# A short-convolution layer: a pinned start with adaLN in pairs of tiles, another plan of passes, sums seeded in PSUM, 1024-wide evictions

## The chip, the cores and the metric

The kernel runs on one core of a Trainium2 chip. The metric is the time of one execution in microseconds on the device. The core has TensorE (PE, with its weight loads shown apart as PEld), VectorE (DVE), ScalarE (ACT), GpSimd (POOL) and SyncE (SP, whose queue issues nearly all loads). The engines run their own instruction streams in order and wait for each other by semaphores.

## What is computed

One layer with depth 1, so only the short gated convolution is used. D is 2048 features, E 4096 channels, 256 tokens, all in float32.

```python
h = rmsnorm(x, norm_g[0])
mod = silu(c) @ ada_w[0] + ada_b[0]              # 2048 x 6144
shift, scale, gate = split(mod, 3)
h = h * (1 + scale) + shift
b_gate, c_gate, v, g = split(h @ sc_w_in[0], 4)  # 2048 x 16384
u = causal_depthwise_conv(c_gate * v, sc_conv_w[0])   # width 3
y = b_gate * u * silu(g)
out = rmsnorm(x + gate * (y @ sc_w_out[0]), final_g)  # 4096 x 2048
```

## The kernel before, in words

**Products.** PE multiplies in a form that takes numbers of reduced width in one pass (`fp32r`). To keep the exactness of float32, each operand is split into two parts that sum to it: `split` makes `hi` on ACT (a cast) and `lo = raw - hi` on DVE for every piece of weights, and the tokens lie in `hT` as a high half `hh_` and a low half `hl_`. A product of a 128 x 128 block of weights and 256 tokens is then three matmuls: `hi` with `hh`, `hi` with `hl`, `lo` with `hh`. They are called products here.

**The start.** x is loaded by token tiles, normalised, and turned by PE (`tp_x`) so that its features lie on partitions, in `xs`. adaLN's shift and scale are a product of a single vector with a 2048 x 4096 matrix. It is done on DVE: a piece of `ada_w` (`at`) is multiplied by `silu_c`, one number per partition, and added to `gv` (L236, L238); then PE turns `gv` (`tp_g`, L247), ACT sums along the rows (L249), and DVE makes `scale` and `shift` (L251 to L253). Features come in 16 tiles of 128. `ADA` lists how many tiles' columns come together. When a group's scale and shift are known, `xs` is modulated (L258) and split into `hT` (L261, L262).

**First stage.** So that PE has work while adaLN's matrix streams in, the first 16 channel tiles are cut along the contraction: 4 chunks of 4 channel tiles, each with its four quarters of `w_in` (the order is `QUARTERS`). A call of `part` is one pass: it takes, for one chunk and quarter, the products of feature tiles `k0` to `k1`, collected in two banks `mm_s`, and copies the sum to `acc` (ACT, L298) or adds it there (DVE, L300). `plan()` writes down the order of passes and of adaLN's pieces before anything runs, from a count of loads and products. Before the change it gives 56 passes, 16 of them first ones and 40 that add.

**Second stage.** The other 16 channel tiles go two at a time over all features: `mm_b`, where one matmul takes `hi` with both halves of a feature tile's tokens (512 wide, L382) and a second `lo` with `hh` (L385). Gate columns of `ada_w` (`at_g`) are summed meanwhile. **Third stage.** The product with `w_out` (`mm_o`, L426 to L428), four chunks of 512 columns, each for two token tiles, then the gated residual (`gated`) and the last norm (`finish`). In the last chunk three pieces' products of the second token tile are put off (`late`), so that the first tile's residual and norm run beside them.

**What sets the order.** Python's order gives priorities; a scheduler with a model of the engines' times then sets each engine's order and the semaphores. Tiles come from pools with a fixed number of buffers (`raw` 3, `hi` and `lo` 3 each, `at` 4, PSUM `mm` 6 banks and `sm` 2), and a load waits on SP's queue until its buffer is free; what stands behind it on the queue waits too.

Of the kernel before, what the change touches and what calls it, by code (L numbers as in the profile page):

```python
# [13 lines left out]
P = 128  # L14
# [8 lines left out]
# Channel tiles whose products are cut along the contraction, while the adaLN vectors stream in: NCH chunks of  # L23
# CT tiles, each chunk in its four quarters of w_in; the feature tiles that adaLN's vectors come in.
# [7 lines left out]
BEHIND = 20  # L32
DELAY = 80
PRODUCTS = 1.7
# Numbers per partition of a piece of w_in or w_out and of a piece of ada_w; slots of CT * T numbers.
# [4 lines left out]

def plan():
    """The order of the start: ("ada", k0, nk, i) loads the i-th piece of the columns of adaLN's feature tiles k0 to
    k0 + nk, ("mm", chunk, quarter, k0, k1) takes the products of feature tiles k0 to k1 for a part of the channels.
    A unit is the load of one 128 x 128 block."""
    steps, ready = [], []
    parts = [(ch, q) for ch in range(NCH) for q in QUARTERS]
    done = {p: 0 for p in parts}
    pieces = [(sum(ADA[:g]), nk, i) for g, nk in enumerate(ADA) for i in range(4 * nk)]
    load, pe = 32.0, 0.0

    def ada():
        nonlocal load
        k0, nk, i = pieces.pop(0)
        steps.append(("ada", k0, nk, i))
        load += 8
        if i == 4 * nk - 1:
            ready.extend([load + DELAY] * nk)

    def take(p, hi):
        nonlocal load, pe  # L60
        n = (hi - done[p]) * CT
        steps.append(("mm", *p, done[p], hi))
        load += n
        pe = max(pe, ready[hi - 1], load + 16 - n) + n * PRODUCTS
        done[p] = hi

    for _ in range(4 * ADA[0]):
        ada()
    while any(done[p] < KT for p in parts):
        while pieces and load + 8 < pe - BEHIND:  # L70
            ada()
        new = [p for p in parts if done[p] == 0]
        hi = sum(r <= max(pe, ready[0]) for r in ready)
        if new:
            take(new[0], hi)
            continue
        old = [p for p in parts if done[p] < KT]
        p = old[0] if hi == KT else min(old, key=lambda p: done[p])
        if hi == done[p]:
            while len(ready) == hi:  # L80
                ada()
            pe = ready[hi]
            hi = sum(r <= pe for r in ready)
        take(p, hi)
    return steps
# [3 lines left out]
def short_conv_layer(ctx: ExitStack, tc: tile.TileContext, x, c, norm_g, ada_w, ada_b, w_in, conv_w, w_out, final_g, out):  # L89
# [6 lines left out]
    psum = ctx.enter_context(tc.tile_pool(name="psum", bufs=6, space=PSUM))  # L96
# [12 lines left out]
    rows1 = const.tile([80, P], F32, tag="rows1", name="rows1")  # L109
    rows2 = const.tile([96, P], F32, tag="rows2", name="rows2")  # L110
    nc.sync.dma_start(rows1[0:16, :], c.rearrange("o (k p) -> (o k) p", p=P))
    xt = [raw_tile(f"x{t}") for t in range(TT)]
    for t in range(TT):
        for dh in range(2):
            dd = slice(dh * (D // 2), (dh + 1) * (D // 2))
            nc.sync.dma_start(xt[t][:, dd], x[t * P : (t + 1) * P, dd])
    nc.sync.dma_start(rows1[16:32, :], norm_g.rearrange("o (k p) -> (o k) p", p=P))
    nc.sync.dma_start(rows1[32:80, :], ada_b.rearrange("o (k p) -> (o k) p", p=P))
# [8 lines left out]
    vec = const.tile([P, 80], F32, tag="vec", name="vec")  # L127
# [3 lines left out]
    def turn(rows, n, lo, dst):  # L131
        tp = psum.tile([P, 512], F32, tag="sm", name="tp_v", bufs=2)
        nc.tensor.transpose(tp[:, : n - lo], rows[lo:n, :], ident[lo:n, lo:n])
        nc.vector.tensor_copy(dst, tp[:, : n - lo])

    turn(rows1, 16, 0, vec[:, 0:16])
    silu = nc.scalar.activation(silu_c, vec[:, 0:16], AF.Silu)

    # The square root's table is fetched before the squares' sum asks for it.
    warm = const.tile([P, 1], F32, tag="warm", name="warm")  # L140
    root = nc.scalar.activation(warm, eps_t, AF.Sqrt)
    tc.add_manual_dep(root.ins, silu.ins.name, after, reason="one change of table")

# [1 line left out]
    ssq = const.tile([P, 2, TT], F32, tag="ssq", name="ssq")  # L145
    rstd = const.tile([P, TT], F32, tag="rstd", name="rstd")
    junk = hpool.tile([P, SLOT], F32, tag="big", name="junk")
    for t in range(TT):
        for dh in range(2):
            dd = slice(dh * (D // 2), (dh + 1) * (D // 2))  # L150
            sq = nc.scalar.activation(junk[:, dd], xt[t][:, dd], AF.Square, accum_out=ssq[:, dh, t : t + 1])
            tc.add_manual_dep(sq.ins, root.ins.name, after, reason="one change of table")
# [3 lines left out]
    for dh in range(2):  # L156
        dd = slice(dh * (D // 2), (dh + 1) * (D // 2))
        for t in range(TT):
            if t == 0:
                nc.scalar.activation(xt[t][:, dd], xt[t][:, dd], AF.Copy, scale=rstd[:, t : t + 1])  # L160
            else:
                nc.vector.tensor_scalar_mul(xt[t][:, dd], xt[t][:, dd], rstd[:, t : t + 1])
# [8 lines left out]
    for k in range(0, KT, 2):  # L171
        tp = psum.tile([P, 2, T], F32, tag="sm", name="tp_x", bufs=2)
        for i in range(2):
            for t in range(TT):
                nc.tensor.transpose(tp[:, i, t * P : (t + 1) * P], xt[t][:, (k + i) * P : (k + i + 1) * P], ident)
        nc.scalar.copy(xs[k // CT][:, k % CT : k % CT + 2, :], tp)
    turn(rows1, 80, 0, vec)
    gT = vec[:, 16:32]
    b_shift = vec[:, 32:48]
    b_scale = vec[:, 48:64]  # L180
    nc.sync.dma_start(rows2[:, :], conv_w.rearrange("w (k p) -> (w k) p", p=P))
    turn(rows2, 96, 0, cw)
# [3 lines left out]

    def split(raw, n):
        """raw = hi + lo, exactly, each of them a number that one pass carries."""
# [5 lines left out]

    def conv(ct, u, cv):
        """u = causal convolution of cv over time, one channel per partition."""
# [11 lines left out]

# [1 line left out]
    acc = {}  # L210
    gjunk = const.tile([P, P], F32, tag="gjunk", name="gjunk")
    adas = ada_w[0].rearrange("(k p) (s f) -> p k s f", p=P, s=3)

    sums = {}
# [298 lines left out]
```

## Time and profile before

| what | value |
|---|---|
| time, median of 3 runs | 952.5 us (952.2 to 952.86) |
| profiled execution, span from first to last instruction | 951.9 us (no other time of it is given) |
| TensorE clock granted, mean over the span | 0.989 |
| read from HBM | 224.49 MB, 238 GB/s over the span |
| PE's last product of the third stage | starts at 942.7 us |

The page gives busy times per engine and the costliest groups of instructions; a table of stretches gives, for each stretch of time, the busy time and the number of instructions of each engine, the clock that TensorE was granted (1.00 is full) and the load rate. The time between the starts of two instructions of a kind, and not their busy time, says how fast PE goes, since its matmuls overlap.

### The profile page before, as it was taken

The numbers are of one execution on the slowest core, as the hardware profiler recorded it, in microseconds if no ns is written. First come the engines' busy times: TensorE is split into PE (matmuls) and PEld (weight loads), VectorE is DVE, ScalarE is ACT, GpSimd is POOL, SyncE is SP. The second block draws the span as 40 slices with busy tenths as digits, with TensorE's granted clock in tenths as the row PEclk, the third lists the DMA queues.
The fourth block names the chain that finished last, engine by engine and source line by source line (L and its number), as shares of the span: only waits on it lengthen the run. The fifth ranks groups of instructions, "written<-read, shape, count | busy, mean of one in ns | idle before, by whom it ended". The sixth has DMA issues, their size and how long they took to land.

```text
span 951.9 us, 14329 instructions
## 1 busy us (share of the span) xinstructions
PE 917.5 (96%) x5963; PEld 834.8 (88%) x5963; DVE 667.7 (70%) x785; ACT 418.2 (44%) x468; POOL 0.7 (0%) x6
## 2 busy tenths in 40 slices
PE   3699999999999999999999999999999999999996
PEld 2699999999999999988888888888888878888884
DVE  4798998899899998997565556556555654454533
ACT  6575342443435444444443544444444433433332
POOL 0000000000000000000000000000000000000000
PEclk9799999999999999999999999999999999999998
DMA  9999997999988887886655665565556585665532
GB/s 271 298 360 368 283 337 251 326 329 321 366 296 290 256 261 237 281 298 200 198 195 178 193 203 179 185 199 190 177 184 201 191 309 180 198 198 177 180 130 88
DMA packets 172048, 227.51 MB, mean 239 GB/s; under 512 B 5792, under 2 KB 112464, under 8 KB 171600
## 3 DMA queue, kind: packets, MB, share of 16 engines
q1 hardware_dynamic: 171984, 226.61, 73.0%
q8 instruction: 46, 0.75, 0.3%
q14 instruction: 18, 0.15, 0.0%
HBM read 224.49 MB, written 2.10 MB: 238 GB/s over the span
## 4 chain that ended last, share of the span: by engine, by line
PE 90%; DMA 4%; DVE 3%; issue 1%; ACT 1%; SPq 1%; ACTq 0%; DVEq 0%
PE mm_b L382 25%; PE mm_b L385 13%; PE mm_s L292 11%; PE mm_s L286 11%; PE mm_s L291 11%; PE mm_o L427 6%; PE mm_o L426 6%; PE mm_o L428 6%; DMA raw_s<-in_sc_w_in_dram 2%; DMA at<-in_ada_w_dram 2%; DVE lo L192 1%; DMA x<-in_x_dram 1%; DVE gv L238 1%; ACT hi L191 0%; SPq L231 0%
## 5 line engine op out<-in xcount | busy, mean ns | idle before, releaser
L382 PE MATMUL mm_b<-hT,hi 128*128 128x512 f32 x1024 | 355.2, 392 | 0.0
L286 PE MATMUL mm_s<-hT,hi 128*128 128x256 f32 x1024 | 286.9, 284 | 9.2 <-ACT hT L261 4.9
L291 PE MATMUL mm_s<-hT,hi 128*128 128x256 f32 x1024 | 287.2, 283 | 0.0
L385 PE MATMUL mm_b<-hT,lo 128*128 128x256 f32 x1024 | 285.4, 280 | 0.0
L292 PE MATMUL mm_s<-hT,lo 128*128 128x256 f32 x1024 | 282.9, 283 | 1.4 <-DVE lo L192 1.3
L192 DVE TENSOR_TENSOR lo<-raw,hi 128x2048 fp32r<-128x2048 f32 x64 | 146.6, 2291 | 128.4 <-ACT hi L191 128.3
L382 PEld LDWEIGHTS mm_b<-hT,hi 128*128 128x128 f32 x1024 | 192.1, 188 | 42.3 <-issue 0.2
L191 ACT CAST hi<-raw_s 128x2048 fp32r<-128x2048 f32 (+3 forms) x85 | 126.5, 1489 | 177.5 <-PE mm_s L291 120.7
L286 PEld LDWEIGHTS mm_s<-hT,hi 128*128 128x128 f32 x1024 | 194.3, 191 | 10.2 <-ACT hT L261 5.1
L291 PEld LDWEIGHTS mm_s<-hT,hi 128*128 128x128 f32 x1024 | 195.1, 191 | 0.2 <-issue 0.2
L292 PEld LDWEIGHTS mm_s<-hT,lo 128*128 128x128 f32 x1024 | 191.9, 190 | 2.3 <-DVE lo L192 2.1
L385 PEld LDWEIGHTS mm_b<-hT,lo 128*128 128x128 f32 x1024 | 192.3, 188 | 0.5 <-issue 0.2
L191 ACT CAST hi<-raw 128x2048 fp32r<-128x2048 f32 x64 | 122.4, 1912 | 158.0 <-PE mm_b L382 103.1
L192 DVE TENSOR_TENSOR lo<-raw_s,hi 128x2048 fp32r<-128x2048 f32 (+3 forms) x85 | 149.5, 1759 | 19.7 <-ACT hi L191 19.2
L192 DVE TENSOR_TENSOR lo<-raw_o,hi 128x2048 fp32r<-128x2048 f32 x32 | 73.4, 2292 | 85.4 <-ACT hi L191 85.4
L191 ACT CAST hi<-raw_o 128x2048 fp32r<-128x2048 f32 x32 | 61.2, 1913 | 105.1 <-PE mm_o L428 92.3
L427 PE MATMUL mm_o<-lo,y 128*128 128x512 f32 x256 | 101.8, 399 | 0.0
L426 PE MATMUL mm_o<-hi,y 128*128 128x512 f32 x256 | 101.0, 396 | 0.0
L428 PE MATMUL mm_o<-hi,y 128*128 128x512 f32 x256 | 100.1, 392 | 0.0
L238 DVE SCALAR_TENSOR_TENSOR gv<-at,silu_c,gv 128x512 f32<-128x512 f32 (+1 forms) x149 | 92.2, 639 | 2.6 <-DMA at<-in_ada_w_dram 1.9
L426 PEld LDWEIGHTS mm_o<-hi,y 128*128 128x128 f32 x256 | 48.1, 188 | 12.6 <-issue 0.2
L428 PEld LDWEIGHTS mm_o<-hi,y 128*128 128x128 f32 x256 | 48.1, 188 | 11.5
(80 smaller groups left out, 441.8 us busy)
## 6 DMA issues: line engine op xcount, KB each, us to landing
raw<-in_sc_w_in_dram SPq DMA_DIRECT2D x64, 1024.0 KB, 5.6
raw_s<-in_sc_w_in_dram SPq DMA_DIRECT2D x46, 1024.0 KB, 7.5
at<-in_ada_w_dram SPq DMA_DIRECT2D x128, 256.0 KB, 6.6
raw_o<-in_sc_w_out_dram SPq DMA_DIRECT2D x32, 1024.0 KB, 5.1
at_g<-in_ada_w_dram SPq DMA_DIRECT2D x32, 512.0 KB, 6.8
raw_s<-in_sc_w_in_dram SPq DMA_DIRECT2D x19, 512.0 KB, 5.8
raw_s<-in_sc_w_in_dram SPq DMA_DIRECT2D x7, 768.0 KB, 7.6
raw_s<-in_sc_w_in_dram SPq DMA_DIRECT2D x13, 256.0 KB, 4.5
```

The costliest lines, as they stand in the source:

```text
L191: nc.scalar.copy(hi[:, :n], raw[:, :n])
L192: nc.vector.tensor_tensor(out=lo[:, :n], in0=raw[:, :n], in1=hi[:, :n].bitcast(F32), op=ALU.subtract)
L238: nc.vector.scalar_tensor_tensor(out=g2, in0=at4[:, i], scalar=c_k, in1=g2, op0=ALU.mult, op1=ALU.add)
L286: first = nc.tensor.matmul(dst, hi[:, o], hh, start=opens, stop=False, skip_group_check=True)
L291: nc.tensor.matmul(dst, hi[:, o], hl, start=False, stop=False, skip_group_check=True)
L292: nc.tensor.matmul(dst, lo[:, o], hh, start=False, stop=k == k1 - 1, skip_group_check=True)
L382: nc.tensor.matmul(banks[m].rearrange("p a t -> p (a t)"), hi[:, o], hT[:, k, :], start=k == 0, stop=False, skip_group_check=True)
L385: nc.tensor.matmul(banks[m][:, 0, :], lo[:, o], hh_[:, k], start=False, stop=k == KT - 1, skip_group_check=True)
L426: nc.tensor.matmul(po, yh, hi[:, o], start=ct == 0, stop=False)
L427: nc.tensor.matmul(po, yh, lo[:, o], start=False, stop=False)
L428: nc.tensor.matmul(po, yl, hi[:, o], start=False, stop=ct == NCT - 1)
```

## The change

- **Start.** All instructions of the start are pinned in the order in which they are written (`in_order`), and what comes behind may be tied to their ends (`behind`). The small loads of vectors go to ACT's queue. x comes first on SP, then adaLN's columns of the first two feature tiles in pieces of 4, 4, 4, 2, 1 and 1 row blocks, with the first weights ahead of the last piece. x lies in four slots of its own. Half of the squares are done on DVE. Only the first four feature tiles of x are scaled and turned in the start; the others follow behind the passes number 4, 7 and 10 (`turn_x`). `idle(n)` has PE turn `ident` n times without use between the loads' landings, 104 times in all.
- **adaLN.** Eight groups of two tiles. The sum over partitions is a matmul with a column of ones, and its result is read from PSUM; three of the first group's 16 row blocks are taken by PE instead of DVE (`ON_PE`). `hT`'s high half is made by ACT straight from `xs` with scale and bias; DVE modulates `xs` beside it for the low half.
- **Plan.** `plan()` counts in microseconds for loads, PE, DVE and ACT, and gives 51 passes: 16 first ones (12 with two feature tiles, then four with four) and 35 that add. Each says whether it is seeded; all 35 are.
- **Seeds.** A seeded pass first has ACT copy `acc` into the pass's PSUM tile, PE adds to it, and ACT copies the sum back. No DVE addition is left.
- **1024-wide tiles in PSUM.** `mm` has three tiles of two banks each, evicted by one instruction. In the third stage the two token tiles share one such tile (`both`).
- adaLN's sums and the gate's sums get a later priority (`later`).

```diff
-ADA = [1, 1, 1, 1, 2, 2, 2, 2, 2, 2]
+ADA = [2] * 8
...
+    steps, ready = [], [0.0] * ADA[0]
...
+        products((hi - done[p]) * CT, ready[hi - 1])
+        seed = done[p] > 0 and act < dve
...
-    psum = ctx.enter_context(tc.tile_pool(name="psum", bufs=6, space=PSUM))
+    psum = ctx.enter_context(tc.tile_pool(name="psum", bufs=3, space=PSUM))
...
+    @contextmanager
+    def in_order():
+        traced = nc.cur_bb.bb.instructions
+        n = len(traced)
+        yield
+        last = {}
+        for ins in list(traced[n:]):
+            if ins.engine in last:
+                tc.add_manual_dep(ins, last[ins.engine], after, reason="in order")
+            last[ins.engine] = ins.name
+        ended.update(last)
...
+    GIVE = 300
+    IDLE = (16, 30, 24, 14, 14, 6)
+    xt = [[slot([P, HX], f"x{t}{dh}") for dh in range(2)] for t in range(TT)]
...
+    nc.scalar.dma_start(rows0[:, :], c.rearrange("o (k p) -> (o k) p", p=P))
...
+    for n, (j, kk) in enumerate(((0, 4), (4, 4), (8, 4), (12, 2), (14, 1), (15, 1))):
...
+        if j == KT - 1:
+            raw0 = raw_tile("raw0")
+            first_load(raw0, 0)
+        for s in range(2):
+            nc.sync.dma_start(at[:, :, s, :], adas[:, j : j + kk, s, 0 : NK0 * P])
...
+    def idle(n):
+        for _ in range(n):
+            nc.tensor.transpose(tp_idle[:, 0, 0:P], ident, ident)
...
+    def turn_x(k0, k1, vector=False):
+        c0, n = k0 % 8 * P, (k1 - k0) * P
+        x0, x1 = (xt[t][k0 // 8][:, c0 : c0 + n] for t in range(TT))
+        nc.scalar.activation(x0, x0, AF.Copy, scale=rstd[:, 0:1])
...
+    def modulate(k0, nk, sums):
...
+            nc.vector.tensor_tensor(out=scale[:, ks], in0=sums[1], in1=b_scale1[:, ks], op=ALU.add)
+            nc.vector.tensor_tensor(out=scale[:, ks], in0=scale[:, ks], in1=gT[:, ks], op=ALU.mult)
+            nc.vector.tensor_tensor(out=shift[:, ks], in0=sums[0], in1=b_shift[:, ks], op=ALU.add)
+        for k in range(k0, k0 + nk):
+            hf = xs[k // CT][:, k % CT, :]
+            nc.scalar.activation(hh_[:, k], hf, AF.Identity, bias=shift[:, k : k + 1], scale=scale[:, k : k + 1])
...
+    for k in range(KT):
+        c_k = silu_c[:, k : k + 1]
+        if k in ON_PE:
+            idle(IDLE[2 + ON_PE.index(k)])
+            sum0(k, first_ada[k], c_k)
...
-        for o in range(2 * nk):
-            nc.tensor.transpose(tp[:, o, :], gv[:, o // nk, (o % nk) * P : (o % nk + 1) * P], ident)
-        for o in range(2 * nk):
-            nc.scalar.activation(gjunk, tp[:, o, :], AF.Copy, accum_out=gs[:, o : o + 1])
...
+            nc.tensor.matmul(
+                ps[:, o : o + 1], gv[:, o // nk, (o % nk) * P : (o % nk + 1) * P], ones[:, 0:1], start=True, stop=True, skip_group_check=True
             )
...
+    def keep(ch, q, k0, bank, seed=False):
+        if k0 == 0 or seed:
+            if k0 == 0:
+                acc[ch, q] = slot([P, CT, T], f"acc{ch}{q}")
+            nc.scalar.copy(acc[ch, q], bank)
+        else:
+            nc.vector.tensor_tensor(out=acc[ch, q], in0=bank, in1=acc[ch, q], op=ALU.add)
...
+        bank = psum.tile([P, CT, T], F32, tag="mm", name="mm_s")
+        if seed:
+            nc.scalar.copy(bank, acc[ch, q])
...
+            if step[2] == 0 and len(acc) in LATER:
+                k = 4 + 4 * LATER.index(len(acc))
+                with tc.issue_after(last_mm[0].ins), behind(ended):
+                    turn_x(k, k + 4)
...
-            for m in range(2):
-                nc.scalar.copy(z[:, m, :], banks[m][:, 1, :])
-                nc.vector.tensor_tensor(out=z[:, m, :], in0=banks[m][:, 0, :], in1=z[:, m, :], op=ALU.add)
+            nc.scalar.copy(z, bank[:, :, 1, :])
+            nc.vector.tensor_tensor(out=z, in0=bank[:, :, 0, :], in1=z, op=ALU.add)
...
-        po = [psum.tile([P, 512], F32, tag="mm", name="mm_o") for _ in range(TT)]
+        both = psum.tile([P, TT, 512], F32, tag="mm", name="mm_o")
+        po = [both[:, t] for t in range(TT)]
```

How the change moves instructions is shown at three places. The first is SP's queue at the start, before (x and the vectors are ahead; `at` are adaLN's pieces, `raw_s` weights):

```order
L231 DMA at_180<-in_ada_w_dram 128x4x128 x2
L231 DMA at_187<-in_ada_w_dram 128x4x128 x2
L231 DMA at_194<-in_ada_w_dram 128x4x128 x2
L231 DMA at_201<-in_ada_w_dram 128x4x128 x2
L273 DMA raw_s<-in_sc_w_in_dram 128x512
L231 DMA at<-in_ada_w_dram 128x4x128 x8
L273 DMA raw_s<-in_sc_w_in_dram 128x512 x3
L231 DMA at<-in_ada_w_dram 128x4x128 x2
L273 DMA raw_s<-in_sc_w_in_dram 128x512
```

and now, behind x:

```order
L204 DMA at_94<-in_ada_w_dram 128x4x256 x2
L204 DMA at_97<-in_ada_w_dram 128x2x256 x2
L204 DMA at_100<-in_ada_w_dram 128x256 x2
L170 DMA raw_104<-in_sc_w_in_dram 128x512
L204 DMA at_103<-in_ada_w_dram 128x256 x2
L170 DMA raw_104<-in_sc_w_in_dram 128x512
L448 DMA raw_s<-in_sc_w_in_dram 128x2x512 x2
L380 DMA at<-in_ada_w_dram 128x2x256 x8
L448 DMA raw_s<-in_sc_w_in_dram 128x2x512 x2
```

The first group is twice as wide, and weights for three passes stand ahead of the next group's first eight loads, where one piece stood before.

The second place is DVE just behind the first group's sums, before (`xs` and `hT` are the modulated tokens, `lo` the low part of weights):

```order
L253 SCALAR_TENSOR_TENSOR scale<-scale,vec 128x1
L238 SCALAR_TENSOR_TENSOR gv<-at,silu_c,gv 128x2x128
L258 TENSOR_SCALAR xs_117<-xs_117,scale,shift 128x256
L238 SCALAR_TENSOR_TENSOR gv<-at,silu_c,gv 128x2x128
L192 TENSOR_TENSOR lo<-raw_s,hi 128x512
L238 SCALAR_TENSOR_TENSOR gv<-at,silu_c,gv 128x2x128
L262 TENSOR_TENSOR hT<-xs_117,hT 128x256
```

and now, where the two tiles' `xs` and `hT` and the first weights' `lo` are pinned together:

```order
L303 TENSOR_TENSOR shift<-sum_195,vec 128x2
L307 TENSOR_SCALAR xs_189<-xs_189,scale,shift 128x256
L310 TENSOR_TENSOR hT<-xs_189,hT 128x256
L307 TENSOR_SCALAR xs_189<-xs_189,scale,shift 128x256
L310 TENSOR_TENSOR hT<-xs_189,hT 128x256
L317 TENSOR_TENSOR lo<-raw_104,hi 128x512
L391 TENSOR_SCALAR gv<-at,silu_c 128x512
L317 TENSOR_TENSOR lo<-raw_s,hi 128x1024
L393 SCALAR_TENSOR_TENSOR gv<-at,silu_c,gv 128x512 x4
L317 TENSOR_TENSOR lo<-raw_s,hi 128x1024
```

The next group's adaLN steps no longer stand between the first group's own steps, but one stands ahead of the second pass's `lo` and four ahead of the third's.

The third place is PE's end of the last column chunk, before, where the first token tile's last products are those with `y_4637` and the late ones of the second tile follow:

```order
L428 MATMUL mm_o<-hi,y_4637 128x512
L426 MATMUL mm_o<-hi,y_4637 128x512
L427 MATMUL mm_o<-lo,y_4637 128x512
L428 MATMUL mm_o<-hi,y_4637 128x512
L428 MATMUL mm_o<-hi,y_4634 128x512
L426 MATMUL mm_o<-hi,y_4634 128x512
```

and now, with each row's waits (`y_4549` is the first tile's last block):

```order
L591 MATMUL mm_o<-hi,y_4549 128x512
L592 MATMUL mm_o<-lo,y_4549 128x512
L593 MATMUL mm_o<-hi,y_4549 128x512
L591 MATMUL mm_o<-hi,y_4544 128x512 [waits DVE_49]
L592 MATMUL mm_o<-lo,y_4544 128x512
L593 MATMUL mm_o<-hi,y_4544 128x512
```

All 36 late products now stand behind the first tile's last one, and the first of them waits for DVE.

More of the change, by code (lines that the diff above doesn't have):

```diff
@@ L38 @@
 NSLOT = KT // CT + 4 * NCH
[L41 to L49 removed]
+LOAD = 0.19
+ALOAD = 1.55
+PRODUCTS = 0.356
+VBLOCK = 0.143
+VPIECE = 1.5
+VSUM = 1.22
+SBLOCK = 0.119
+SCOPY = 1.03
+SSEED = 2.05
+WLAG = 6.0
+ALAG = 8.0
+WAHEAD = 14.0
+AAHEAD = 6.0
+def plan():
+    steps, ready = [], [0.0] * ADA[0]
+    done = {}
+    pieces = [(sum(ADA[:g]), nk, i) for g, nk in enumerate(ADA) if g for i in range(4 * nk)]
+    load, pe, dve, act = 0.0, 4.0, 0.0, 0.0
+    burst = SLOT // P
@@ L65, in take @@
         done[p] = hi
-    for _ in range(4 * ADA[0]):
+    while pieces:
         ada()
[L69 to L84, printed above, removed]
```

292 lines of the change are left out of this document (187 added, 105 removed).

## The prediction

> **What bounds the kernel now.** I read the page's busy times first.
>
> ```profile
> PE 917.5 (96%) x5963; PEld 834.8 (88%) x5963; DVE 667.7 (70%) x785; ACT 418.2 (44%) x468; POOL 0.7 (0%) x6
> ```
>
> PE carries the kernel. Its busy time overlaps itself (matmuls are pipelined), so it cannot show a slow clock. Counting instructions per stretch can: next is the table of stretches for the instructions of `mm_s` alone, the products of the first 16 channel tiles (columns: stretch, its length, busy time and count on PE, PEld, DVE and ACT, granted clock, DMA share, GB/s).
>
> ```profile
> 27.10:30.60 3.50, 3.45 (x16) 3.46 (x17) 0.00 (x0) 0.59 (x1) 0.51 0.97 255
> 30.60:37.50 6.90, 6.90 (x58) 6.72 (x57) 0.00 (x0) 4.72 (x9) 1.00 0.87 255
> 37.50:42.10 4.60, 0.06 (x2) 0.02 (x1) 0.00 (x0) 0.16 (x1) 0.86 1.04 357
> 42.10:47.60 5.50, 5.47 (x24) 5.17 (x25) 0.00 (x0) 0.90 (x2) 0.50 1.08 301
> 47.60:60.00 12.40, 11.60 (x96) 11.24 (x96) 0.00 (x0) 4.55 (x8) 1.00 1.08 354
> 60.00:80.00 20.00, 20.00 (x169) 19.84 (x168) 0.00 (x0) 4.58 (x8) 1.00 1.07 371
> 80.00:400.00 320.00, 317.73 (x2659) 315.58 (x2658) 50.65 (x76) 2.35 (x4) 1.00 0.90 297
> ```
>
> At 60 to 80 us a product costs 20.00/169 = 0.1183 us. From 27.1 to 80 us there are 365 of them (16+58+2+24+96+169), worth 43.2 us, in 52.9 us: 9.7 us are lost. From 80 to 400 us 2659 products are worth 314.6 of 320 us, and the rest is nearly filled by PE's other instructions. From there on nothing is to be won:
>
> ```profile
> 410.00:943.10 533.10, 533.05 (x2804) 454.62 (x2802) 299.23 (x273) 222.08 (x209) 0.00 (x0) 1.00 0.58 191
> ```
>
> That row counts all instructions (POOL's busy time stands before the clock). PE is busy 533.05 of 533.10 us, and the change leaves these products as they are. So the change can win the time before the first product, the 9.7 us behind it, and little else. What ended the waits, from PE's waits and then from the timeline:
>
> ```profile
> PE mm_s L286 <- ACT hT L261: 4.9, 1, 4.9
> PE mm_s L286 <- ACT hi L191: 4.3, 1, 4.3
> PE mm_s L292 <- DVE lo L192: 1.3, 2, 0.8
> ```
>
> ```profile
> 27.15 0.58 PE L286 MATMUL mm_s<-hT,hi 128*128 128x256 f32 x1 [4.88 <-ACT hT L261]
> 42.08 0.58 PE L286 MATMUL mm_s<-hT,hi 128*128 128x256 f32 x1 [4.33 <-ACT hi L191]
> 55.00 0.38 PE L292 MATMUL mm_s<-hT,lo 128*128 128x256 f32 x1 [0.80 <-DVE lo L192]
> 40.98 1.04 ACT L191 CAST hi<-raw_s 128x1024 fp32r<-128x1024 f32 x1 [4.21 <-DMA raw_s<-in_sc_w_in_dram]
> ```
>
> The first product starts at 27.15 us. At 42.08 PE had run out of work that one feature tile allows, since weights queued behind adaLN's loads. Each time the clock was then about 0.5 for several microseconds: 16 products in 3.5 us, 24 in 5.5. The rest of 0.80 us at 55.00 did not slow it.
>
> **The first product (removed: one tile; added: two).** The new start loads x (2.1 MB), the columns of two tiles (16 row blocks, 512 columns, 4.19 MB) and the first weights (0.26 MB). The rows of vectors leave SP for ACT's queue.
>
> ```profile
> 0.74 0.39 SPq L111
> 2.59 7.61 DMA x<-in_x_dram
> ```
>
> ```profile
> 10.00:20.00 10.00, 5.48 (x29) 1.00 1.16 297
> ```
>
> x landed at 10.20; without the 0.45 us that L111 holds SP, 9.75. The next 4.46 MB go at 297 GB/s (that row, 512-byte pieces) at worst and at 371 (60 to 80 us, longer pieces) at best: 15.0 or 12.0 us. I take 330, since 1024-byte pieces lie between: 13.5 us, last landing at 23.25. Meanwhile DVE needs 13 x 0.745 = 9.7 us for its sums (three row blocks go to PE), so it keeps up. Behind the landing come six one-column matmuls at no more than 0.11 each (0.66), three small DVE steps of 0.15 with handing over (about 0.75), ACT's `hT` at 0.405, and some 0.5 us of hand-overs: 2.3. The first product starts at about 25.6: **-1.5 us** (from -3.0 to 0). The pinned table loads, squares, scalings and first eight transposes end near 15 us (x at 9.75, then some 5.5 of ACT, DVE and PE) and are hidden by that landing; a landing before 15 us would bare them. ACT issues its four loads (1.6 us at 0.39 each) ahead of its first table load, and x's first quarter lands behind both. Of the 104 idle turns only the last six (0.7) come behind the last landing, beside DVE's and ACT's steps.
>
> ```profile
> 91.43 0.44 PE tp_g L247 x4
> ```
>
> ```profile
> L238 DVE SCALAR_TENSOR_TENSOR gv<-at,silu_c,gv 128x512 f32<-128x512 f32 x90 | 66.3, 745 | 2.4 <-DMA at<-in_ada_w_dram 1.9
> L261 ACT CAST hT<-xs 128x256 fp32r<-128x256 f32 x16 | 5.9, 405 | 5.1 <-DVE xs L258 4.9
> L262 DVE TENSOR_TENSOR hT<-xs,hT 128x256 fp32r<-128x256 f32 x16 | 6.3, 416 | 0.0
> L258 DVE TENSOR_SCALAR xs<-xs,scale,shift 128x256 f32<-128x256 f32 x16 | 6.0, 408 | 0.0
> L192 DVE TENSOR_TENSOR lo<-raw_s,hi 128x1024 fp32r<-128x1024 f32 x19 | 23.2, 1219 | 4.4 <-ACT hi L191 4.1
> L191 ACT CAST hi<-raw_s 128x1024 fp32r<-128x1024 f32 x19 | 20.0, 1051 | 37.4 <-PE mm_s L291 24.0 <-DMA raw_s<-in_sc_w_in_dram 6.6 <-DVE gv L238 3.4
> L191 ACT CAST hi<-raw_s 128x2048 fp32r<-128x2048 f32 x46 | 88.0, 1913 | 109.7 <-PE mm_s L291 72.0 <-DMA raw_s<-in_sc_w_in_dram 19.4 <-issue 11.5
> L298 ACT COPY acc<-mm_s 128x512 f32<-128x512 f32 x32 | 17.9, 597 | 8.4 <-PE mm_s L292 8.1
> L300 DVE TENSOR_TENSOR acc<-mm_s,acc 128x512 f32<-128x512 f32 x80 | 53.3, 683 | 4.2 <-PE mm_s L292 4.1
> ```
>
> **The 9.7 us lost.** Two tiles give each of the first twelve passes 24 products, 2.84 us, where one gave 1.42. So the run of work behind the first product is 34 us and not some ten, and the wait that ended at 42.08 goes, with the half clock behind it. The transposes of `ident` at the start are put there between loads. If the clock is full at the first product, all goes: **-9.7 us**.
>
> **What is late next, at the start.** The first product of `hl` needs `xs` and `hT` on DVE (0.408 + 0.416) behind ACT's `hT`: 0.8 us of PE. On DVE an adaLN step that waits for its landing stands ahead of the second pass's `lo` (1.219). It lands 1.83 MB behind the last columns, some 5.1 us, at 28.3; that `lo` ends near 30.0, and PE asks at 29.2: 0.8. Four adaLN steps (3.0) stand ahead of the third pass's `lo`: 34.2 against 32.9: 1.3. Together **+2.9 us** (from 0, if the landings are early and overlap, to 6, if each of three `lo` comes a further 1 us late).
>
> **Transposes moved.** Of the 32 transposes of x, 24 now run among the products, with one turn of `rows2`. Ahead of the first product they cost PE nothing; here 24 x 0.11 + 0.3 = **+2.9 us**, the price of a full-clock transpose. The six scalings that feed them stand on ACT (3.6 us at L298's 0.597) ahead of the third pass's `hi`; they end before DVE gets there, and the third pass's `lo` stays the later one. DVE no longer scales x behind the start.
>
> **Sums.** 32 turns and 64 ACT entries go; 28 one-column matmuls come behind the start. The turns held PE 32 x 0.11 = 3.5 us. For a one-column product no row exists: at most 0.11, at least about a quarter of that; nearest in form is the turn, but it streams 128 columns, so I take 0.07: **-1.5 us** (-2.7 to -0.4).
>
> **Later groups of tiles.** Seven follow, in place of nine. Each has a chain from sums to `hl` while DVE has a 2048-wide `lo` and two adaLN steps in between, some 5 to 6 us, against 5.7 us of products that are there. Nine groups now cost 1.3 us of waits on `lo`, 0.15 each. I take twice that, since each group now holds two tiles: 2.1, less the 0.5 that lies outside the 9.7: **+1.6 us** (-0.5 to +6, where every chain is 0.9 late).
>
> **Seeds.** Of 51 passes 35 add to earlier ones; all are seeded: ACT copies `acc` into PSUM, PE adds, ACT copies back. DVE loses 80 x 0.683 = 54.6 us; that is hidden now and worth nothing directly. ACT gains 35 copies each way at about 1.05 (nearest row: L191 of 1024; 2 x 0.597 bounds it above). Where a pass has four tiles, ACT needs 1.913 + 2 x 1.05 = 4.0 of its 5.7 us; three tiles of PSUM let a seed be made two passes ahead. So **0**; without that cover 35 x 1.05 = 36.8 us.
>
> **1024-wide evictions.** The last two stages have the same products, and a bank pair rests two passes before it is used again: 0. One place differs. The last column chunk's two banks are now one tile, and the late products of the second half wait for DVE's read of the first:
>
> ```profile
> 937.96 0.69 DVE L472 TENSOR_TENSOR big<-mm_o,gate 128x512 f32<-128x512 f32 x1 [7.43 <-PE mm_o L428]
> 937.99 0.39 PE L426 MATMUL mm_o<-hi,y 128*128 128x512 f32 x1
> ```
>
> Now PE goes on beside that read; then it stands for 0.69 and a hand-over: **+0.75 us** (0.7 to 1.0). Behind it 36 late products still cover the first half's finish.
>
> **Sum.** 951.9 - 1.5 - 9.7 + 2.9 + 2.9 - 1.5 + 1.6 + 0.75 = 947.3 us of span. The median of the runs, 952.5, is 0.6 above the span: 947.9.
>
> **Rivals.**
>
> *A cold clock at the first product.* The clock falls soon after PE rests:
>
> ```profile
> 22.00:24.00 2.00, 0.26 (x2) 0.93 1.17 290
> 24.00:26.00 2.00, 0.00 (x0) 0.50 1.10 348
> ```
>
> The last turn ran at 21.8, and the clock fell within 24 us. In the new start the third piece is in at 19.3 (3.15 MB behind x), sums and 14 idle turns end at 21.2, and PE rests some 2 us until the last landing; one-column matmuls may count for little. Price: 16 products in 3.5 us lost 1.6 and 24 in 5.5 lost 2.7; waits on DVE overlap some: +1.8, so 949.7.
> The Trainium skill, "TensorE: Matmul & The Clock Gate", section "Why this matters for your kernels", holds that only rests above about 3 us bring the half clock back. By that rule this rival falls away, and the forecast stands. The trace does not agree: here less than 2 us of rest sufficed, behind sparse work, and the trace decides.
>
> *Seeds on the path (slower).* Should each seeded pass expose its seed's wait by 0.3 us, because ACT works in order and a copy back waits for PE ahead of the next `hi`, that is +10.5: 958.4. It reaches "slower" (954.4) from 0.19 us a pass. For it: four of the passes have two tiles, where ACT needs 3.15 of 2.84 us. Against it: the others leave 1.7 us or more each, and ACT is below half busy now.
>
> *Loads bound the first passes (no change).* Twelve passes with their 28 adaLN pieces take 6.3 + 7.3 MB: 36.7 us at 371 GB/s, just PE's 34 + 2.9. At 310 it is 43.9: +7.2 less the 2.9 of waits it covers, and the first product 0.9 later: about 953.1. The rate of 371 from 60 us on speaks against it, the 297 at the start for it.
>
> *No new waits.* If loads run at 371 and later groups fit, -2.9 and -2.1: 942.9.
>
> **How the numbers follow.** Forecast 0.47, cold clock 0.20, seeds 0.09, loads 0.12, no new waits 0.12. A measurement here can tell about 0.2% (1.9 us) from no change. Faster means below 950.6: nearly all of forecast and "no new waits", most of the cold clock: 0.76. Same: the loads, the rest of the cold clock: 0.13. Slower: seeds, a bad end of the loads: 0.11. The range, 941.5 to 952.5, takes in "no new waits", the cold clock and the ends of the terms, and leaves out the seeds and most of the loads.
>
> **What the new profile would show.** The first product at 24 to 27 us, clock 1.00 there, no rest of 4 us behind it; rests of about 1 us on `lo` before 40 us; from 80 to 400 us no rests on ACT's seeds; at the end one rest of 0.75 us on DVE. I am wrong if PE waits for ACT at many passes, if weights still land late around 40 us, or if the first product comes after 30.

## The result and the profile after

The changed kernel takes 957.93 us (median of 4 runs, 957.79 to 959.22), the kernel before 952.35 (4 runs, 951.62 to 952.86): a ratio of 1.0053, 95% interval 1.004 to 1.0066. It is slower by 5.6 us, where 4.6 us less were forecast. The profiled execution has a span of 956.2 us (before 951.9).

The start did what was said of it. This is the table of stretches of the kernel after, for `mm_s` alone, in the same stretches and columns as before (no VectorE column, since no `acc` is added there):

```profile
27.10:30.60 3.50, 3.50 (x32) 3.50 (x32) 0.00 (x0) 1.00 1.09 383
30.60:37.50 6.90, 6.00 (x50) 5.75 (x49) 3.03 (x3) 1.00 1.03 349
37.50:42.10 4.60, 3.97 (x34) 3.78 (x33) 1.01 (x1) 1.00 1.02 357
42.10:47.60 5.50, 5.50 (x48) 5.45 (x47) 2.02 (x2) 1.00 1.07 388
47.60:60.00 12.40, 11.14 (x92) 10.78 (x92) 4.06 (x4) 1.00 1.03 364
60.00:80.00 20.00, 18.07 (x151) 17.69 (x150) 4.06 (x4) 1.00 1.07 390
```

From 27.1 to 80 us PE now runs 407 products, where it ran 365. The clock is full throughout. The waits of PE's products that are left (waiting engine, who ends the wait; us in total, times, the longest):

```profile
PE mm_s L418 <- DVE lo L317: 2.2, 2, 1.3
PE mm_o L591 <- DVE big L638: 0.8, 1, 0.8
PE mm_s L417 <- DVE hT L310: 0.5, 1, 0.5
PE mm_s L412 <- ACT hT L306: 0.5, 1, 0.5
```

No seed is among them. Yet the gain was gone at the end. The timeline shows the stages' first products and the last one (start, length):

```profile
25.43 0.38 PE L412 MATMUL mm_s<-hT,hi 128*128 128x256 f32 x1 [0.49 <-ACT hT L306]
...
403.36 0.39 PE L548 MATMUL mm_b<-hT,hi 128*128 128x512 f32 x1
...
766.01 0.40 PE L591 MATMUL mm_o<-hi,y 128*128 128x512 f32 x1
...
946.86 0.40 PE L593 MATMUL mm_o<-hi,y 128*128 128x512 f32 x1
```

and before:

```profile
406.92 0.40 PE L382 MATMUL mm_b<-hT,hi 128*128 128x512 f32 x1
...
763.27 0.80 PE L426 MATMUL mm_o<-hi,y 128*128 128x512 f32 x1
...
942.66 0.39 PE L428 MATMUL mm_o<-hi,y 128*128 128x512 f32 x1
```

The second stage begins 3.6 us earlier and ends 2.7 us later: it takes 362.65 us, where it took 356.35. PE does not wait in it. Per stretch, for `mm_b` alone (columns: length, PE, PEld, DVE, ACT, clock, DMA share, GB/s), before:

```profile
420.00:740.00 320.00, 319.70 (x1844) 281.08 (x1843) 24.49 (x59) 21.64 (x59) 1.00 0.61 194
```

and after:

```profile
420.00:740.00 320.00, 319.71 (x1809) 277.23 (x1808) 19.31 (x29) 16.19 (x28) 1.00 0.59 188
```

The busy time is equal, the clock is full, and yet 35 fewer of the same matmuls start (1.9%). The timeline shows where. After:

```profile
499.81 0.40 PE L548 MATMUL mm_b<-hT,hi 128*128 128x512 f32 x1
500.05 0.28 PE L551 MATMUL mm_b<-hT,lo 128*128 128x256 f32 x1
500.17 0.39 PE L548 MATMUL mm_b<-hT,hi 128*128 128x512 f32 x1
500.40 0.28 PE L551 MATMUL mm_b<-hT,lo 128*128 128x256 f32 x1
500.52 0.40 PE L548 MATMUL mm_b<-hT,hi 128*128 128x512 f32 x1
```

From the start of the 512-wide matmul to the next start it is 0.24 us, then 0.23, then 0.24. Up to the gate's sums at 719.94 us it is 229 ns for even feature tiles and 240 ns for odd ones, and 117 and 121 ns for the 256-wide matmul behind it; the two together are a *pair* below. Behind these sums it is the even tiles that take 240 ns. So every second pair is slow, whichever tile it belongs to. Before, the medians are 229 to 230 and 117 to 118 ns for all.

Nothing in these instructions differs but where their operands lie. The change took tiles out of the constants' pool and put others in, and what lies behind it in SBUF begins 64 bytes lower per partition (`raw`, `hi` and `lo` also changed their order there, by steps that are multiples of 256): the weights `hi` and `lo` start at an address of 0 modulo 256 after, at 64 before. `hT` starts at 224 in both. I call *distance* the address of `hT` less that of the weights, modulo 256: 160 before, 224 after. The tiles in PSUM changed too, from one bank to two.

### The profile page after: what moved, and what is told of

Read it like the earlier page. It is cut to its first block, busy times and chain, and to the rows that moved or that the text cites. A ratio compares the mean times of both kernels' runs of the same rounds, so it can differ in the third digit from the quotient of the medians.

```text
span 956.2 us, 14443 instructions
## 1 busy us (share of the span) xinstructions
PE 938.4 (98%) x6123; PEld 850.9 (89%) x6123; DVE 617.4 (65%) x628; ACT 469.0 (49%) x423; POOL 0.7 (0%) x6
## 4 chain that ended last, share of the span: by engine, by line
PE 95%; DMA 2%; DVE 1%; SPq 1%; ACT 0%; issue 0%; ACTq 0%; DVEq 0%
PE mm_b L548 25%; PE mm_b L551 13%; PE mm_s L418 12%; PE mm_s L412 12%; PE mm_s L417 12%; PE mm_o L591 6%; PE mm_o L593 6%; PE mm_o L592 6%; DMA at<-in_ada_w_dram 1%; DMA x<-in_x_dram 1%; SPq L204 0%; PE sum_g L399 0%; DVE lo L317 0%; PE ps_gate L528 0%; PE tp_x L286 0%
## 5 line engine op out<-in xcount | busy, mean ns | idle before, releaser
L548 PE MATMUL mm_b<-hT,hi 128*128 128x512 f32 x1024 | 362.3, 397 | 0.0
L418 PE MATMUL mm_s<-hT,lo 128*128 128x256 f32 x1024 | 288.5, 282 | 2.2 <-DVE lo L317 2.2
L317 DVE TENSOR_TENSOR lo<-raw,hi 128x2048 fp32r<-128x2048 f32 (+1 forms) x66 | 148.1, 2243 | 143.8 <-ACT hi L316 143.8
L316 ACT CAST hi<-raw 128x2048 fp32r<-128x2048 f32 (+1 forms) x66 | 123.2, 1867 | 185.2 <-issue 89.5
L317 DVE TENSOR_TENSOR lo<-raw_s,hi 128x2048 fp32r<-128x2048 f32 (+1 forms) x78 | 147.6, 1892 | 55.5 <-ACT hi L316 52.3
L316 ACT CAST hi<-raw_s 128x2048 fp32r<-128x2048 f32 (+1 forms) x78 | 124.2, 1592 | 106.8 <-PE mm_s L417 81.8
L393 DVE SCALAR_TENSOR_TENSOR gv<-at,silu_c,gv 128x512 f32<-128x512 f32 x105 | 78.5, 748 | 3.6 <-DMA at<-in_ada_w_dram 1.4
L426 ACT COPY acc<-mm_s 128x1024 f32<-128x1024 f32 x51 | 51.4, 1010 | 28.5 <-PE mm_s L418 28.5
L591 PEld LDWEIGHTS mm_o<-hi,y 128*128 128x128 f32 x256 | 48.0, 187 | 13.0 <-DVE big L638 1.2
```

Source lines behind the costliest of these rows:

```text
L316: nc.scalar.copy(hi[:, :n], raw[:, :n])
L317: nc.vector.tensor_tensor(out=lo[:, :n], in0=raw[:, :n], in1=hi[:, :n].bitcast(F32), op=ALU.subtract)
L393: nc.vector.scalar_tensor_tensor(out=gv, in0=at4[:, i], scalar=c_k, in1=gv, op0=ALU.mult, op1=ALU.add)
L418: last_mm[0] = nc.tensor.matmul(dst, lo[:, o], hh, start=False, stop=k == k1 - 1, skip_group_check=True)
L426: nc.scalar.copy(acc[ch, q], bank)
L548: nc.tensor.matmul(bank[:, m].rearrange("p a t -> p (a t)"), hi[:, o], hT[:, k, :], start=k == 0, stop=False, skip_group_check=True)
```

## The experiments

Three theories were set up. A: the place of the weights in SBUF sets the pace. B: the two-bank tiles in PSUM do. C: the place of instructions in PE's stream does. In all kernels with unused bytes, PE's instructions and their order are those of the kernel they start from.

**64 bytes back.** The kernel after, with

```diff
+    pad = const.tile([P, 16], F32, tag="pad", name="pad"); nc.vector.memset(pad, 0.0)
     eps_t = const.tile([P, 1], F32, tag="eps", name="eps_t")
```

> The changed kernel with 64 bytes per partition of unused constants ahead of the weight tiles, so that they lie at the byte address modulo 128 (64) that they had before; the instructions stay. Theory A (the place of the weight tiles in SBUF sets how fast the products of the second stage go): a start-to-start of 229 and 117 ns for every pair L548, L551, in place of 240 and 121 ns for every second feature tile; the 1024 such pairs slowed save 1024 x (11 + 4) ns, or by the sums of the intervals 8.5 us, so 949 to 950 us. Theory B (two banks of PSUM to a tile, or their numbers, slow them) and theory C (the place of the instructions in PE's stream): nothing changes, 957.9 +- 1 us.

Measured: 952.65 us, ratio to before 0.9994 (0.9984 to 1.0004): the slowdown is gone. Second stage:

```profile
420.00:740.00 320.00, 319.70 (x1843) 280.98 (x1842) 19.83 (x29) 16.06 (x28) 1.00 0.60 192
```

The pace is that of before, 230/228 and 117/118 ns, and theory A's mechanism holds. The time misses its 949 to 950. The stage gained 6.8 us and not 8.5: the mean interval of a pair went from 353.3 to 346.7 ns, over 1024 pairs. And this execution lost 1.7 us of it at the start, of which more below.

**The same 64 bytes in the kernel before.**

> The kernel before with the same 64 bytes, which put its weight tiles at a byte address modulo 128 of 0, as in the changed kernel. Theory A: every second feature tile of the second stage goes at 240 and 121 ns, 952.4 + 8.5 = 960.9 us. Theories B and C: 952.4 +- 1 us, with 229 and 117 ns throughout.

Measured: 962.11 us, ratio 1.0097 (1.0081 to 1.0112): 9 us for 64 unused bytes.

```profile
420.00:740.00 320.00, 319.71 (x1826) 278.21 (x1825) 23.78 (x57) 21.27 (x58) 1.00 0.61 194
```

But there is no such alternation: 231/233 and 118 ns for all, and the first stage slowed as well (its median went from 119 to 121 ns). The second stage lost 3.4 us and the first 4.2, where 8.5 were expected in the second alone; that the time comes near 960.9 is luck. So the address modulo 128 is not the rule (0 here and in the kernel after); the distance is 96.

**Evictions and PSUM tiles of the last two stages undone.** A second pool of six one-bank tiles replaces the three two-bank tiles behind the first stage:

```diff
-            bank = psum.tile([P, 2, 2, T], F32, tag="mm", name="mm_b")
+            banks = [pmm2.tile([P, 2, T], F32, tag="mm", name="mm_b") for _ in range(2)]
...
-        both = psum.tile([P, TT, 512], F32, tag="mm", name="mm_o")
-        po = [both[:, t] for t in range(TT)]
+        po = [pmm2.tile([P, 512], F32, tag="mm", name="mm_o") for _ in range(TT)]
```

> The changed kernel with the evictions of the last two stages undone: PSUM tiles of one bank each and 512-wide evictions there, as before; the first stage keeps its two-bank tiles and the weight tiles keep their place. Theory A: 240 and 121 ns stay for every second feature tile; only the waits of the last stage on a tile that is shared by two halves go (0.8 us before the late products, 1.2 us in all), and the pools' change between the stages may cost up to 2 us: 956 to 959 us. Theory B: 229 and 117 ns throughout and 949 us or less. Theory C: as A.

Measured: 962.34 us, ratio 1.0102 (1.0086 to 1.0118), slower than my range. 229 and 240 ns stay, so theory B falls. Here the even feature tiles are the slow ones from the start, at the same addresses and with the same order of PE's instructions in this stage, so the tile's own address does not say which pair is slow. The pools' change cost 3.5 us, where up to 2 were allowed for; it waits for the first stage's last copy to `acc`:

```profile
408.21 0.50 PE L548 MATMUL mm_b<-hT,hi 128*128 128x512 f32 x1 [3.45 <-ACT acc L426]
```

The wait before the late products went, as expected. The first product came at 26.45 us instead of 25.43, and the clock was 0.56 from 27.10 to 30.60 us, where the kernel after had 1.00.

**Sums turned instead of one-column products.**

```diff
         for o in range(2 * nk):
-            nc.tensor.matmul(
-                ps[:, o : o + 1], gv[:, o // nk, (o % nk) * P : (o % nk + 1) * P], ones[:, 0:1], start=True, stop=True, skip_group_check=True
-            )
+            nc.tensor.transpose(ps[:, o * P : (o + 1) * P], gv[:, o // nk, (o % nk) * P : (o % nk + 1) * P], ident)
+        nc.vector.reduce_sum(gs[:, 0 : 2 * nk], ps[:, 0 : 2 * nk * P].rearrange("p (o f) -> p o f", f=P), axis=mybir.AxisListType.X)
```

> The changed kernel with the sums over partitions of the seven later groups turned by PE (four transposes to a group) and summed by one reduction on VectorE, in place of four products with a single column (0.79 us a group on PE in the trace). The weight tiles move by 128 bytes, so their address modulo 128 stays 0. If the one-column products cost what their records show: 7 x (0.79 - 4 x 0.11) = 2.45 us less, 955.5 us. Rival: their time lies in PE's pipeline beside the products, and nothing is gained, 957.9. By theory A the second stage keeps 240 and 121 ns; had the place modulo 256 mattered, it would change here, by up to 8.5 us.

Measured: 958.83 us, ratio 1.0064 (1.0051 to 1.0076): no gain in time. In the trace, though, PE's time between the products of the first stage went from 5.4 to 2.4 us for the sums, 3.0 less, and the waits of 0.3 us and more from 3.7 to 3.2. What took it back was the moved weights and the start. The first product came 0.8 us later, and the clock was 0.54 from 27.10 to 30.60 us (17 products instead of 32). The distance is 96 here. The second stage lost its alternation (233/231 and 118 ns, 3.4 us less), but a product of the first stage takes 120.0 ns instead of 118.3, some 5 us more. A run that moves tiles by an unheeded 128 bytes cannot size 3 us.

**`hT` moved instead of the weights, 64 bytes.** A pool of unused bytes lies above `hT`; the slots below it (`y` among them) move along.

```diff
+    rightp = ctx.enter_context(tc.tile_pool(name="rightp", bufs=1, side="right"))
     hpool = ctx.enter_context(tc.tile_pool(name="hpool", bufs=1, side="right"))
...
+    hpad = rightp.tile([P, 16], F32, tag="hpad", name="hpad"); nc.vector.memset(hpad, 0.0)
```

> The changed kernel with the normalised activations hT (and the slots below them) 64 bytes lower, at an address modulo 128 of 32 in place of 96; the weight tiles stay at 0. Theory A1 (what counts is how the moving operand hT lies to the weights, which is then as it was before: 32 apart modulo 128): 229 and 117 ns for all pairs of the second stage, 6.3 us less in it than in the changed kernel. Theory A2 (the place of the weight tiles alone counts): 240 and 121 ns stay for every second feature tile, the time stays at 957.9 +- 1.

Measured: 950.21 us (one run; before 953.07 on the same chip). The weights stand where the kernel after has them, and the pace is that of before, 230/228 and 117/118 ns:

```profile
420.00:740.00 320.00, 319.71 (x1843) 280.98 (x1842) 19.14 (x28) 16.63 (x29) 1.00 0.60 192
```

So it is how the two lie to each other that counts, and theory A1 stands against A2. The slots moved with `hT`; that `hT` is the one that matters is argued, from PE reading none of the slots in these products. Theory C falls with it, here and in the first run: PE's instructions are the same throughout.

**`hT` 96 bytes lower (24 numbers in `hpad`).**

> The changed kernel with hT 96 bytes lower, at an address modulo 128 of 0, as the weights. Theory A2: 240 and 121 ns stay. Theory A1 says only that it is neither the old nor the changed distance; a third theory (A3: a row of hT that starts 32 bytes before a multiple of 128 costs an extra access) expects all products faster, for 512 columns between 213 ns (512 columns at the 107 ns per 256 columns that half of the slow 213 ns makes) and 229 ns, which would be 8 to 16 us over the kernel's 1024 pairs.

Measured: 955.77 us (one run), 233 and 120 ns for both kinds of feature tile: neither the old pace nor the changed one, as A1 allows. A start of `hT` at a multiple of 128 brings nothing by itself; A3 falls.

**32 bytes ahead of the weights (8 numbers in `pad`).**

> The changed kernel with 32 bytes of unused constants ahead of the weight tiles, which lie at an address modulo 128 of 32 then; hT stays at 96. Theory A2 with a step at 64 bytes (an address is good or bad by its 64-byte half): as the changed kernel, 229 and 240 ns by turns. Theory A1: a distance of 64 modulo 128, not seen so far. If the pace is one more value, between 229 and 240 ns, the pace depends on the address in steps of 32 bytes.

Measured: 946.68 us (one run), the fastest so far. The second stage goes at 235 and 118 ns, but a product of the first stage takes some 115 ns on average, where the kernel after has 118.3. So 32 bytes are enough to change the pace, and the stages differ in what suits them.

**160, 192 and 224 bytes ahead of the weights (40, 48 and 56 numbers).**

> The changed kernel with its weight tiles 160 bytes higher: distance hT minus weights 64 modulo 256. If the distance counts modulo 128, this repeats the distance of 192: 235 and 118 ns in the second stage, about 115 ns in the first, 946.7 us. If it counts modulo 256 (distances 96 and 224 differ in the runs so far, 231 to 233 against 229 and 240 ns), another value, between 229 and 240 ns and 944 to 960 us.

> The changed kernel with its weight tiles 192 bytes higher: distance hT minus weights 32 modulo 256. Modulo 128 this repeats the distance of 160: 229 and 117 ns, 952 us (950.2 to 952.7 seen there). Modulo 256: another value, 944 to 960 us.

> The changed kernel with its weight tiles 224 bytes higher: distance hT minus weights 0 modulo 256. Modulo 128 this repeats the distance of 128: 231 and 120 ns, 955.8 us. Modulo 256: another value, 944 to 960 us.

Measured: 953.46, 948.34 and 959.58 us (one run each; before 954.36 there). Two of the three nearly repeat in the second stage what was seen 128 bytes away (228 and 118 ns at 32, as at 160; 233 and 119 at 64, near the 235 and 118 at 192). The third does not (235 and 117 at 0, 233 and 120 at 128), nor did 96 and 224, and the last stage differs between 64 and 192. So modulo 128 is not the rule. All eight distances in steps of 32, with the number of products that start in a fixed stretch of each stage:

| distance | kernel | `mm_s`, 85 to 385 us | `mm_b`, 420 to 740 us | `mm_o`, 775 to 920 us | time, us |
|---|---|---|---|---|---|
| 0 | after, weights +224 | 2443 | 1810 | 638 | 959.6 |
| 32 | after, weights +192 | 2510 | 1843 | 620 | 948.3 |
| 64 | after, weights +160 | 2536 | 1809 | 619 | 953.5 |
| 96 | after, sums turned | 2466 | 1825 | 617 | 958.8 |
| 128 | after, `hT` -96 | 2471 | 1821 | 622 | 955.8 |
| 160 | after, weights +64 | 2473 | 1843 | 619 | 952.7 |
| 192 | after, weights +32 | 2544 | 1808 | 631 | 946.7 |
| 224 | after | 2478 | 1809 | 620 | 957.9 |

The spread is 4% in the first stage, 2% in the second and 3% in the third (where the weights are the moving operand and `y` the stationary one), and 13 us in all. The times hold the start too, which differed from run to run (11 to 32 products between 27.10 and 30.60 us), and five of them are of one run; the counts leave the start out. At 96 the turned sums leave the products some 2 us more of the first window. No distance is best everywhere: 192 is best in the first stage and among the worst in the second.

Different kernels at the same distance agree in the second stage: 1844 (before) and 1843 (weights +64, `hT` -64, and the kernel with three parts mended) at 160, 1826 (before with 64 bytes) and 1825 at 96, 1809 (evictions undone) and 1809 at 224, 1809 (the last kernel below) and 1808 at 192. In the first stage the agreement is looser: 2473 with the weights moved and 2486 with `hT` and the slots moved, both at 160, so the distance is not all that counts there.

**Three parts mended.** Sums turned (the tiles of their results take 64 bytes, so the distance is 160), and a tile for each half of the last stage's rows:

```diff
-        both = psum.tile([P, TT, 512], F32, tag="mm", name="mm_o")
-        po = [both[:, t] for t in range(TT)]
+        po = [psum.tile([P, TT, 512], F32, tag="mm", name="mm_o")[:, 0] for t in range(TT)]
```

> The changed kernel with three of its parts mended: the weight tiles at their old address modulo 128 (by the 64 bytes that the two new tiles of sums take), the seven later sums turned by PE and reduced by VectorE, and a tile of its own in PSUM for each half of the output's rows. From the run with 64 bytes (952.65 us, before 953.15): sums 5.4 to 2.4 us and the waits around them 1.1 to 0.9 as in the trace with turns, so -3.0 to -3.3; the two waits of 0.8 and 1.2 us in the last stage go, -1.5 to -2.0. So 947.3 to 948.2 us, 0.5% under the kernel before. If the sums' time was hidden: 950.7; if the last stage's waits come back as others: 949.5.

Measured: 947.91 us, ratio to before 0.9942 (0.9927 to 0.9957), as expected. Against the kernel with 64 bytes, whose distance is the same, the first stage is 3.2 us shorter (375.6 against 378.7) and the last 1.1 (179.8 against 180.9).

**The same at a distance of 192 (one tile of 32 bytes for the sums' results).**

> The kernel with the three mended parts (947.91 us), its weight tiles 32 bytes lower: the distance hT minus weights, modulo 256, is 192 in place of 160. From the run at that distance and the one at 160 that differ in nothing else (946.68 and 952.65 us): 6 us less, 941.5 to 942.5 us; first stage at a mean near 115 ns a product in place of 118.5, second stage at 235 and 118 ns in place of 229 and 117, last stage at 229 in place of 233 ns. If what the 32 bytes gain depends on the rest of the kernel, it stays between 945 and 948.

Measured: 943.02 us, ratio 0.9873 (0.9849 to 0.9897): 1.3% under the kernel before. The first stage takes 367.6 us (375.6 at 160), the second 362.7 (355.8), the last 176.4 (179.8): 4.5 us less, where 6 were expected.

## Why the prediction was wrong, point by point

Against the span, -4.6 us was forecast and +4.3 measured, a miss of 8.9. Counted from the starts of PE's instructions, it falls into these steps:

| step | forecast | measured |
|---|---|---|
| first product | -1.5 | -1.7 (27.15 to 25.43 us) |
| losses up to 80 us, less the new early stalls | -6.8 | -6.1 (waits 6.8 to 3.7, matmuls at half clock 3.0) |
| transposes moved | +2.9 | +2.4 |
| sums | -1.5 | +2.8 |
| waits of the later groups | +1.6 | -0.8 |
| gate's sums and products' pace in the first stage | 0 | -0.1 |
| second stage | 0 | +6.3 |
| last stage | +0.75 | +1.5 |

**The step that failed** is "The last two stages have the same products", and with it "the change leaves these products as they are". The instructions are the same, but their operands are not where they were. The +6.3 us is the product's own pace, shown by the 64 bytes in both kernels and by moving `hT` and the slots alone. The row that was to show that nothing changes there, PE busy for 533.05 of 533.10 us, cannot show a pace: after the change PE is as busy in the second stage (319.71 of 320 us) and slower. The signs that were named for the new profile came, and none of them looks at the pace. Without the 6.3 the span would have come out 2.0 us shorter, and not 4.6: the sums' miss of 4.3 is partly made up by the later groups' 2.4 the other way, which is luck. The 1024-wide evictions, which I priced at 0, did cost PE nothing there: undoing them left the pace as it was.

**The sums were mis-sized.** The 28 one-column products were taken at 0.07 us each, bounded by 0.03 and 0.11. The chain shows one group of four:

```profile
89.73 0.79 PE sum_g L399 x8
```

In float32 each stands twice in the trace, 0.11 us a time. So one costs about 0.2 us, and the bound from a transpose's row was no bound, since there each transpose stands once in the trace (four in 0.44 us). All groups together cost 5.4 us, where the turns in the same stretch cost 2.6.

**The later groups** were costed too high, in the other direction: PE has no wait of 0.2 us or more on them behind 80 us. **The tail** waited for VectorE 0.8 us as forecast; the rest of the 1.5 is hand-over and two of the gate's sums, which now fall into the last stage.

**The rivals.** Seeds on the path: no. ACT copies back 51 times at 1.01 us, and PE waits for no seed:

```profile
L426 ACT COPY acc<-mm_s 128x1024 f32<-128x1024 f32 x51 | 51.4, 1010 | 28.5 <-PE mm_s L418 28.5
```

It would have given the right sign for a wrong reason. Loads bound the first passes: no, they went at 349 to 390 GB/s. "No new waits": by half; the later groups fitted, but waits came up to 80 us (3.3 us, 2.9 forecast). Cold clock at the first product: not in the profile of the kernel after, but in those of all eleven kernels made from it by the experiments, with a clock of 0.50 to 0.68 from 27.10 to 30.60 us and 11 to 23 products where the kernel after has 32. In the kernel with 64 bytes the instructions on PE are the same. Its pieces of `ada_w` landed later:

```profile
22.45 1.05 PE L329 MATMUL sum<-silu_c,at 128*128 128x1 f32 x8 [0.23 <-DMA at<-in_ada_w_dram]
24.08 1.05 PE L329 MATMUL sum<-ones,gv 128*128 128x1 f32 x8 [0.57 <-DVE gv L342]
24.99 0.85 PE L232 MATMUL tp_idle<-ident 128*128 128x128 f32 x6
26.34 0.38 PE L412 MATMUL mm_s<-hT,hi 128*128 128x256 f32 x1 [0.50 <-ACT hT L306]
```

and the products that followed went at half clock:

```profile
27.10:30.60 3.50, 3.35 (x15) 3.35 (x16) 0.00 (x0) 0.51 1.10 350
```

15 products stand where the kernel after has 32; by 80 us it is 402 against 407. The first product came 0.9 us later and the first stage took 0.8 us longer, together the 1.7 us lost. The load rate alone does not set it. With `hT` 96 bytes lower the first product came at 24.95 us and the loads ran nearly as fast as in the kernel after, and the clock fell:

```profile
27.10:30.60 3.50, 3.50 (x23) 3.50 (x23) 0.00 (x0) 0.68 1.08 378
```

The mean clocks of the other executions tell a part of it. In the kernel with 64 bytes all eleven have 0.993 to 0.995, by estimate over 8 us at half clock; the end of the run takes 3.8 to 6.9 of these in the twelve traces, so each of the eleven was cold for a while elsewhere too. The four of the kernel after have 0.995 or 0.996, which does not settle it. How much of the medians this makes stays open, and so does what brings it on. The rule of the Trainium skill weighed in the prediction ("TensorE: Matmul & The Clock Gate", "Why this matters for your kernels": rests above about 3 us) does not agree with the trace of the kernel with 64 bytes either: from 14 us on no rest of PE was over 0.6 us there.

The median of the kernel after stands 1.7 us over its profiled span, that of before 0.5. In every run whose time and span both stand on record, the time is 1.7 to 1.9 us above the span. So the profiled execution of before, whose own time is not on record, was by estimate some 1.3 us slower than that kernel's median. That is the difference between the +4.3 of the spans and the +5.6 of the medians.

## What to carry to other kernels

When a change touches the allocation of anything in SBUF, the products that it "leaves as they are" may go faster or slower, here by up to 4%: compare the number of instructions that start in a fixed stretch, not the busy time, and look at the operands' addresses before looking for a wait. In an experiment keep the addresses fixed, or the moved tiles hide what is measured. A few unused bytes ahead of the weights may be worth a scan in a kernel that TensorE bounds: here the best and the worst place were 13 us apart, more than the 7.8 us that the first two steps of the table won. Which place is best was not the same for the stages of this one kernel, so no place can be carried over.

## What the runs showed of the hardware

- The start-to-start time of float32r matmuls at full clock, with no wait, depends on how moving and stationary operand lie to each other in SBUF: from 228 to 240 ns for 512 columns, and from 115 to 120 ns on average for the first stage's 256. 32 bytes matter, and the pattern does not repeat after 128 bytes. It repeats after 512: the second stage's weight blocks lie 512 bytes apart and `hT`'s tiles 2048, and the medians are the same for both halves of the channels. Whether it repeats after 256 was not tried.
- At a distance of 224 every second pair is slow (240 and 121 ns, against 229 and 117). The slow tiles change from odd to even behind the gate's sums at 719.94 us, and are the even ones from the start in the kernel with the evictions undone, at the same addresses.
- In eleven of twelve kernels with nearly the same start PE's clock fell to half around the first products (0.50 to 0.68 from 27.10 to 30.60 us); in the kernel with 64 bytes it did so with no rest over 0.6 us from 14 us on.
- The Trainium skill, "SBUF — State Buffer", section "Who interferes with whom", gives PE two read ports, one for the moving operand and one for weight loads, says that they are independent, and that PE never waits on anyone. By that the place should not matter, and the runs do not agree: moving `hT` and the slots by 64 bytes raised the products' rate by 1.9% (1809 to 1843 in 320 us). That the two reads meet somewhere in SBUF would fit, but no run here separates them from the other engines' accesses to the same tiles; the mechanism is argued, the dependence is shown.
- A float32 matmul with one column costs PE 0.2 us here (four in 0.79 us), about twice a 128-column transpose of the same numbers (four in 0.44 us).
